# Queries and keys turned by VectorE and a round trip through HBM, in place of TensorE transposes, in an encoder block

## The chip, the cores and the metric

The kernel runs on one core of a Trainium2 chip, in float32, in one launch. The metric is the device time of one execution in microseconds (us). The median of three runs before the change is 1106.71 us (1106.16 to 1112.32).

Engines are named as in the profile: PE is TensorE (matrix products and transposes), DVE is VectorE, ACT is ScalarE, POOL is GpSimd, SP is SyncE. SP and POOL mostly issue DMA transfers here. Each engine runs its instructions in the order of the program, and waits at an instruction until the data and buffers that it needs are there.

## The reference

The reference is one layer of an encoder for 512 tokens of width 1024. It consists of a half-step feed-forward block, a mixing block with two branches, and a second half-step feed-forward block:

```python
x = x + FFN_RES * _swiglu(_rmsnorm(x, norm_ffn1[l]), w_ffn1_gu[l], w_ffn1_down[l])
h = _rmsnorm(x, norm_mix[l])
xr, gr, q, k, v, ga, gb = jnp.split(h @ w_in[l], splits, axis=-1)
xc = _centred_dwconv(xr, conv_w[l], conv_b[l])
h_fwd = _rglru_scan(xc, ...)            # a recurrence over the tokens, with sigmoid gates
h_bwd = jnp.flip(_rglru_scan(jnp.flip(xc, 1), ...), 1)
y_lru = (h_fwd + h_bwd) * jax.nn.gelu(gr)
q = _rmsnorm(q.reshape(B_, S, N_HEADS, HEAD_DIM), q_norm[l]) * (HEAD_DIM ** -0.5)
k = _rmsnorm(k.reshape(B_, S, N_HEADS, HEAD_DIM), k_norm[l])
y_att = _neighbourhood_attention(q, k, v, rpb[l])   # 16 heads of 64, on an 8 x 64 token grid
y = jax.nn.sigmoid(ga) * y_lru + jax.nn.sigmoid(gb) * y_att
x = x + y @ w_out[l]
x = x + FFN_RES * _swiglu(_rmsnorm(x, norm_ffn2[l]), w_ffn2_gu[l], w_ffn2_down[l])
```

In the attention each token sees a clamped window of 8 rows by 16 columns. A block of 16 query columns is treated against 32 key columns: scores, a bias that also masks, softmax, and the weighted sum of v.

## The kernel before

**Weights and products.** A product in float32 is made of three products of parts: each operand is cut into a high part (a cast) and a low part (the rest). A weight chunk of 128x1024 is loaded by SP into one of three buffers (`wraw`), cut by a cast on ACT (`wh`, line 145; for some chunks on DVE, line 147) and a subtraction on DVE (`wl`, line 148), with four buffers each for `wh` and `wl`, and used by 24 matmuls of 128x512. A merge-gate chunk whose number is odd has its cast on DVE (`f % 2 == 0` in `gates`).

**Order of the work.** PE's order is set by the weight chunks: after (and in the middle of) a chunk `weave` is called, which takes steps from lists of generators, the lanes. A table `RATE` says how many steps of a lane are due per call in each phase. The lanes are `lru` (the recurrence, by a list of numbered steps), `v` (copies of v), `att` (the attention, `heads`) and `tail` (the last applications). `hold` puts an instruction behind the last matmul of the chunk that is current when the step is taken. Within this a scheduler orders each engine's instructions, with `high_priority` for some. The phases are `xr` (input of the recurrence), `t0` (q, k and v of the first eight heads, `hf` 0), `t1` (the same for `hf` 1) and `g` (24 chunks of gates: gelu gate, merge gate A, merge gate B). The first attention half so runs beside the q, k and v chunks of the second, and the second beside the gates.

**q and k.** `tok_group` makes q or k for 128 tokens on the partitions and 512 features: four accumulators (`acc`), four chunks. `qk_raw` copies them from the accumulators on ACT (line 843) into `qk` tiles and takes the sums of squares. In `heads` DVE multiplies by the reciprocal root (line 909). `start(fi)` then handles a pair of heads (`fi` 0 to 3 per half): PE transposes four 128x128 blocks of q (line 918) and four of k (line 920) into `aux` accumulators, ACT makes the scaled high parts `qh` and `kh` (lines 924 and 927), DVE the low parts `ql` and `kl` (lines 926 and 929).

**Scores, softmax, weights.** `scores` issues 12 matmuls (64x256) for one group of query blocks, 24 where both groups are taken together (line 950). DVE adds the bias and takes the minimum of the negated scores (line 970, result `nmx`), ACT the exponentials with their sums (line 977), DVE the reciprocal (line 979) and the multiplication by it (line 982). `ship` turns the weights in 32x32 blocks on DVE (lines 991 and 992) into `pt`, SP stores that to HBM (`pd`), and POOL fetches it back in four transfers into `PT` (line 998). This completes a transposition. `apply` multiplies `PT` with v in 32 matmuls (line 1013). It runs a few units behind: `ATT_LAG` is 4 units for `hf` 0 and 2 for `hf` 1, where a unit is 12 matmuls of scores in `hf` 0 and 24 in `hf` 1.

**v.** v is stored to HBM (`vd`) and fetched back by POOL in shifted forms: `vs` (line 869), and for two edge blocks `va` and `ve` (line 880), six pieces of 64 KB per block, gathered in runs of 64 numbers. `apply` of a half needs all of them.

## Time and profile before

| | before |
|---|---|
| median of 3 runs | 1106.71 us |
| profiled execution | 1114.74 us |
| its span | 1113.0 us |
| granted TensorE clock, mean | 0.995 |
| PE busy | 1102.2 us (99%) |
| DVE busy | 813.4 us (73%) |
| ACT busy | 578.1 us (52%) |
| POOL busy | 148.9 us (13%) |
| bytes moved by DMA | 175.93 MB, 158 GB/s |

The profiled execution took 8.0 us longer than the median; 1.7 us of its time lie outside the span. The busy time of PE counts a matmul from its start to its modelled end, and neighbouring matmuls overlap in it. So a PE that is busy 99% of the time is one that hardly ever has nothing to do, and the time can fall only where PE gets less to do, or where its few idle stretches go. The attention runs beside the chunks from the first transpose at 508.8 us to the end of the last application at 691.4 us of the span.

### The profile page before, as it was taken

How to read it: one execution, taken by the hardware profiler on the slowest of the kernel's cores; microseconds unless marked ns; L12 is line 12 of the kernel's file. 1: busy time of each engine (PE TensorE's matmuls, PEld its weight loads, DVE VectorE, ACT ScalarE, POOL GpSimd, SP SyncE). 2: the span in 40 equal slices, each digit the busy share in tenths (PEclk: the TensorE clock that was granted, in tenths of full speed). 3: DMA queues.
4: the chain of work that ended last, by engine and by line, in shares of the span. 5: the costliest groups of instructions: out<-in, count | busy, mean ns of one | idle time of the engine just before them, and what ended most of it. 6: DMA issues, size and time to landing. Idle time of an engine off the chain costs nothing.

```text
span 1113.0 us, 17676 instructions
## 1 busy us (share of the span) xinstructions
PE 1102.2 (99%) x6811; PEld 976.0 (88%) x6811; DVE 813.4 (73%) x1295; ACT 578.1 (52%) x871; POOL 148.9 (13%) x243
## 2 busy tenths in 40 slices
PE   9999999999999999999999998999999999999998
PEld 7899999988888778788888876889999999998887
DVE  7877777794745776999787974659877777785542
ACT  8554554563533678877354441346655454564330
POOL 0000000000000351230335432001000000000000
PEclk9999999999999999999999998999999999999999
DMA  8566666643423696673796665377766666662421
GB/s 267 154 168 152 155 154 166 165 139 95 134 85 108 166 245 156 173 206 116 205 258 183 205 186 137 101 239 161 198 146 160 157 166 148 158 170 95 133 76 38
DMA packets 64549, 175.93 MB, mean 158 GB/s; under 512 B 14545, under 2 KB 18385, under 8 KB 64465
## 3 DMA queue, kind: packets, MB, share of 16 engines
q1 hardware_dynamic: 43136, 127.75, 35.8%
q0 software_dynamic: 20752, 46.80, 21.5%
q8 instruction: 53, 0.87, 0.3%
q10 hardware_dynamic: 576, 0.26, 0.1%
q14 instruction: 32, 0.25, 0.1%
HBM read 150.53 MB, written 15.73 MB: 149 GB/s over the span
## 4 chain that ended last, share of the span: by engine, by line
PE 95%; issue 2%; DMA 1%; POOL 1%; DVE 0%; ACTq 0%; POOLq 0%; ACT 0%
PE acc L312 31%; PE acc L172 10%; PE acc L173 10%; PE acc L174 10%; PE aux L312 5%; PE acc L831 4%; PE acc L832 4%; PE acc L833 4%; PE aux L172 4%; PE aux L174 4%; PE aux L173 4%; PE aux L742 1%; DMA PT<-pd 1%; POOL PT L998 1%; PE aux L1013 1%
## 5 line engine op out<-in xcount | busy, mean ns | idle before, releaser
L145 ACT ACTIVATE wh<-wraw 128x1024 fp32r<-128x1024 f32 (+3 forms) x224 | 220.7, 987 | 303.7 <-issue 92.1
L148 DVE TENSOR_TENSOR wl<-wraw,wh 128x1024 fp32r<-128x1024 f32 (+3 forms) x236 | 267.3, 1137 | 101.4 <-ACT wh L145 100.3
L312 PE MATMUL acc<-s,wh 128*128 128x256 f32 x1280 | 232.2, 283 | 0.0
L312 PEld LDWEIGHTS acc<-s,wh 128*128 128x128 f32 x1280 | 199.7, 192 | 0.0
L312 PE MATMUL acc<-s,wl 128*128 128x256 f32 x640 | 181.1, 283 | 0.0
L312 PEld LDWEIGHTS acc<-s,wl 128*128 128x128 f32 x640 | 122.9, 192 | 0.0
L172 PE MATMUL acc<-xh,wh 128*128 128x512 f32 x272 | 108.7, 400 | 0.0
L174 PE MATMUL acc<-xh,wl 128*128 128x512 f32 x272 | 107.0, 393 | 0.0
L173 PE MATMUL acc<-xl,wh 128*128 128x512 f32 x272 | 106.9, 393 | 0.0
L312 PE MATMUL acc<-xh,wl 128*128 128x256 f32 x320 | 90.6, 283 | 0.0
L312 PE MATMUL acc<-xl,wh 128*128 128x256 f32 x320 | 90.6, 283 | 0.0
L312 PE MATMUL acc<-xh,wh 128*128 128x256 f32 x320 | 90.5, 283 | 0.0
L831 PE MATMUL acc<-wh,xh 128*128 128x512 f32 x192 | 75.7, 394 | 0.0
L832 PE MATMUL acc<-wh,xl 128*128 128x512 f32 x192 | 74.8, 389 | 0.0
L833 PE MATMUL acc<-wl,xh 128*128 128x512 f32 x192 | 74.7, 389 | 0.0
L148 DVE TENSOR_TENSOR hl<-h,hh 128x512 fp32r<-128x512 f32 x88 | 57.2, 686 | 21.7 <-PE aux L173 21.4
L172 PE MATMUL aux<-hh,wh 128*128 128x512 f32 (+1 forms) x181 | 69.9, 386 | 0.0
L173 PE MATMUL aux<-hl,wh 128*128 128x512 f32 (+1 forms) x181 | 69.9, 386 | 0.0
L174 PE MATMUL aux<-hh,wl 128*128 128x512 f32 (+1 forms) x181 | 69.9, 386 | 0.0
L173 PE MATMUL acc<-hl,wh 128*128 128x512 f32 (+1 forms) x176 | 67.9, 386 | 0.0
L174 PE MATMUL acc<-hh,wl 128*128 128x512 f32 (+1 forms) x176 | 67.9, 386 | 0.0
L172 PE MATMUL acc<-hh,wh 128*128 128x512 f32 (+1 forms) x176 | 67.9, 386 | 0.0
(221 smaller groups left out, 2297.6 us busy)
## 6 DMA issues: line engine op xcount, KB each, us to landing
wraw<-wqkv SPq DMA_DIRECT2D x24, 512.0 KB, 4.9
wraw<-wg SPq DMA_DIRECT2D x24, 512.0 KB, 7.5
wraw<-w1d SPq DMA_DIRECT2D x22, 512.0 KB, 3.7
wraw<-w2s SPq DMA_DIRECT2D x22, 512.0 KB
pair<-w2s SPq DMA_DIRECT2D x22, 512.0 KB, 4.5
wraw<-w2d SPq DMA_DIRECT2D x22, 512.0 KB, 3.7
wraw<-w1s SPq DMA_DIRECT2D x18, 512.0 KB, 3.6
pair<-w1s SPq DMA_DIRECT2D x18, 512.0 KB, 4.9
```

Of the source, the lines that this page charges most:

```text
L145: nc.scalar.activation(H, raw, AF.Copy)
L148: return nc.vector.tensor_tensor(L, raw, H.bitcast(F32), ALU.subtract)
L172: nc.tensor.matmul(ps, wh, xh, start=first, stop=False, skip_group_check=skip)
L173: nc.tensor.matmul(ps, wh, xl, start=False, stop=False, skip_group_check=skip)
L174: mark["mm"] = nc.tensor.matmul(ps, wl, xh, start=False, stop=last, skip_group_check=skip)
L312: mm = nc.tensor.matmul(o, w_[:, c], x_, start=first and m + k == 0 and w_ is H and x_ is xh_, stop=m + k == 4 and w_ is L, skip_group_che ...
L742: prev, mm = mm, nc.tensor.matmul(ps[d][b], W[w][o, c], X[x][o], start=x == 1, stop=w + x == 0)
L831: nc.tensor.matmul(pss[j], xh[kk][:, tj], H[:, s], start=kk == 0, stop=False)
L832: nc.tensor.matmul(pss[j], xl[kk][:, tj], H[:, s], start=False, stop=False)
L833: mark["mm"] = nc.tensor.matmul(pss[j], xh[kk][:, tj], L[:, s], start=False, stop=kk == KT - 1)
L998: nc.gpsimd.dma_start(PT[:, j].rearrange("p q i -> p (q i)"), d[q].rearrange("i c x -> c i x"))
L1013: mm = nc.tensor.matmul(pv[h2 * HD : (h2 + 1) * HD, n * P : (n + 1) * P], vt[:, (fi * 2 + h2) * HD : (fi * 2 + h2 + 1) * HD], PT[:, q], st ...
```

## The change

Five things change together.

1. q and k are no longer turned by PE. A new lane `prep` (`turn_qk`) normalises a tile of q and of k and turns each in 32x32 blocks on DVE into a `pair` tile, which SP stores to HBM (`qd`, four stores of 512 KB per half, in rows of 4 KB). Its steps are due at 1.25 per call in the phases `t0`, `t1` and `g`, so they fall between v's weight chunks. `fetch(qd, fi)` reads a pair of heads back in four transfers on SP (32 partitions by 16 runs of 64 numbers each), into one of two `xqk` buffers. `start(fi)` first issues the fetch for `fi + 1`, and then makes `qh`, `ql`, `kh`, `kl` from `xqk`. The 64 transposes of PE are gone.
2. The norm weight of k is multiplied into that of q (`gq8`), so `kh` and `kl` are made without a scale.
3. The multiplication of the softmax weights by 1/sum moves from DVE to ACT.
4. The casts of all merge-gate and gelu-gate chunks are on ACT; before, every second one was on DVE.
5. The pool of large tiles goes from 43 to 39, and some tiles take other buffers (`ch`, `cl` and part of `th` those of `PT` and `xqk`, `sq` that of `pt`). The rate of `lru` in `t0` goes from 3.25 to 3.

```diff
 RATE = {
-    "t0": {"att": 0.0, "lru": 3.25},
-    "t1": {"att": 0.75, "tail": 0.75, "lru": 2},
-    "g": {"att": 0.7, "tail": 0.7, "lru": 1.5, "v": 0.5},
+    "t0": {"att": 0.0, "lru": 3, "prep": 1.25},
+    "t1": {"att": 0.75, "tail": 0.75, "lru": 2, "prep": 1.25},
+    "g": {"att": 0.7, "tail": 0.7, "lru": 1.5, "v": 0.5, "prep": 1.25},
 }
...
-    gk = small[:, C_KN : C_KN + 1]
+    nc.vector.tensor_tensor(gq8, gq8, small[:, C_KN : C_KN + 1], ALU.mult)
...
-    def heads(hf, raws, st):
+    def turn_qk(raws, st, qd, ahead):
...
-        for w in range(2):
-            for j in range(NCB):
+        for j in range(NCB):
+            t2 = pair_t().rearrange("p a b -> p (a b)")
+            for w in range(2):
                 t = raws[w][j].rearrange("p (h d) -> p h d", d=HD)
                 hold(nc.vector.tensor_tensor(t, t, rq[:, w, j, :].unsqueeze(2).to_broadcast([P, 8, HD]), ALU.mult))
+                nc.vector.transpose(
+                    t2.rearrange("p (c f w i) -> p w f c i", c=NCB, f=4, w=2)[:, w],
+                    raws[w][j].rearrange("p (f c i) -> p f c i", c=NCB, i=32))
+            nc.sync.dma_start(qd[j], t2)
+            yield
+        if ahead:
+            fetch(qd, 0)
+
+    def fetch(qd, fi):
+        t = xs[fi] = big.tile([P, NCB * NCB, 2, 32], F32, tag="xqk", bufs=2, name=nm("xqk"))
+        for c in range(NCB):
+            nc.sync.dma_start(
+                t[c * 32 : (c + 1) * 32].rearrange("p g w i -> p g (w i)"),
+                qd.rearrange("j (a i) c f x -> c f i (j a) x", a=NCB)[c, fi])
+
+    def heads(hf, qd):
+        until("prep", lambda: False)
+        if 0 not in xs:
+            fetch(qd, 0)
             yield
...
         def start(fi):
-            fs = slice(fi * P, (fi + 1) * P)
-            pq, pk = aux_t(), aux_t()
-            for j in range(NCB):
-                hold(nc.tensor.transpose(pq[:, j * P : (j + 1) * P], raws[0][j][:, fs], ident))
-            for j in range(NCB):
-                hold(nc.tensor.transpose(perm(pk)[:, j], raws[1][j][:, fs], ident))
+            if fi < 3:
+                fetch(qd, fi + 1)
+            x = xs.pop(fi).rearrange("p (j a) w i -> p w j a i", j=NCB)
+            xq, xk = x[:, 0], x[:, 1]
...
-            nc.scalar.activation(rev(qh), fwd(pq), AF.Copy, scale=gq8)
+            hold(nc.scalar.activation(rev(qh), xq, AF.Copy, scale=gq8))
...
-            nc.scalar.activation(kh, pk, AF.Copy, scale=gk)
+            hold(nc.scalar.activation(rows(kh), xk, AF.Copy))
             with tc.high_priority():
-                mark["kl"] = nc.vector.scalar_tensor_tensor(kl, pk, gk, kh.bitcast(F32), ALU.mult, ALU.subtract)
+                mark["kl"] = nc.vector.tensor_tensor(rows(kl), xk, rows(kh.bitcast(F32)), ALU.subtract)
...
-                    nc.vector.tensor_scalar(pt, pt, rs[:, hp, n : n + 1], None, ALU.mult)
+                    nc.scalar.activation(pt, pt, AF.Copy, scale=rs[:, hp, n : n + 1])
...
-        lanes["att"].append(heads(hf, raws, st))
+        qd = dram.tile([NCB, P, NCB, 4, 64], F32, tag="qd", bufs=2, name=nm("qd"))
+        lanes["prep"].append(turn_qk(raws, st, qd, hf == 0))
...
+        lanes["att"].append(heads(hf, qd))
...
-            feat_chunk(a["wg3"][w * KT + f], KT, xh, xl, ps, 0, KT, f % 2 == 0, RATE[phase[0]])
+            feat_chunk(a["wg3"][w * KT + f], KT, xh, xl, ps, 0, KT, True, RATE[phase[0]])
```

How this moves the instructions is shown at three places. Numbers at the end of names are those of the tiles.

**First place: PE at the first scores of `hf` 0.** Before, the eight transposes of the first pair of heads (`aux_5186` for q, `aux_5187` for k) are followed by a weight chunk (`wh_5207`), and the scores come behind that:

```order
L918 MATMUL aux_5186<-ident,qk_4444 128x128
L918 MATMUL aux_5186<-ident,qk_4446 128x128
L920 MATMUL aux_5187<-ident,qk_4625 128x8x16
L920 MATMUL aux_5187<-ident,qk_4627 128x8x16
L920 MATMUL aux_5187<-ident,qk_4629 128x8x16
L920 MATMUL aux_5187<-ident,qk_4631 128x8x16
L831 MATMUL acc_5119<-wh_5207,xh_3096 128x512
L832 MATMUL acc_5119<-wh_5207,xl_3097 128x512
```

Now the end of a weight chunk (`wh_5155`) is followed at once by the scores, 24 in a row:

```order
L834 MATMUL acc_4961<-wh_5155,xh_3102 128x512
L835 MATMUL acc_4961<-wh_5155,xl_3103 128x512
L836 MATMUL acc_4961<-wl_5156,xh_3102 128x512
L975 MATMUL aux_5088<-kl_5044,qh_5041 128x256
L975 MATMUL aux_5087<-kl_5044,qh_5041 128x256
L975 MATMUL aux_5088<-kh_5043,qh_5041 128x256
L975 MATMUL aux_5087<-kh_5043,qh_5041 128x256
```

No weight chunk now lies between the work on q and k and the scores; and two units of scores stand together where before a chunk stood between them.

**Second place: ACT at the same point.** Before, the parts of the first pair are made between two weight casts, and then the exponentials of the first unit follow:

```order
L145 ACTIVATE wh_5432<-wraw_5431 128x1024
L924 ACTIVATE qh_5196<-aux_5186,gq_3677 128x4x128
L927 ACTIVATE kh_5198<-aux_5187,small 128x512
L145 ACTIVATE wh_5529<-wraw_5528 128x1024
L977 ACT_TABLE_LOAD
L977 ACTIVATE p_5251,rs_5236<-so_5253,nmx_5254 128x192
```

Now two casts stand directly ahead of `qh` and `kh`. `wh_5467` takes the buffer of `wh_5155`, the chunk that PE uses last before the scores:

```order
L145 ACTIVATE wh_5390<-wraw_5389 128x1024
L145 ACTIVATE wh_5467<-wraw_5466 128x1024
L949 ACTIVATE qh_5041<-xqk_5001,gq_3677 128x4x128
L952 ACTIVATE kh_5043<-xqk_5001 128x4x8x16
L1002 ACTIVATE p_5101,rs_5086<-so_5103,nmx_5104 128x192
L1002 ACTIVATE p_5102,rs_5086<-so_5103,nmx_5104 128x256
```

Behind the four exponentials and four multiplications of that unit come the parts of the second pair, two tanh of the recurrence, and only then the copies out of the accumulators that `wh_5155`'s chunk filled; PE's next chunk writes to these accumulators:

```order
L1007 ACTIVATE p_5101<-p_5101,rs_5086 128x192
L1007 ACTIVATE p_5102<-p_5102,rs_5086 128x256
L949 ACTIVATE qh_5136<-xqk_5036,gq_3677 128x4x128
L952 ACTIVATE kh_5138<-xqk_5036 128x4x8x16
L769 ACTIVATE th_5149<-gate_4806,sp_3673 128x512
L769 ACTIVATE th_5152<-gate_4815,sp_3673 128x512
L846 ACTIVATE qk_5184<-acc_4958 128x512
```

The softmax of a unit has moved ahead of the copies that free the accumulators.

**Third place: POOL in the second half of the attention.** Before, the copies of v's edge blocks (`va`, `ve`) for `hf` 1 stand ahead of its softmax weights (`PT`), but for one piece:

```order
L876 MEMSET ve_6123 128x512
L880 DMA va_6122<-vd_82 64x4x64 x2
L880 DMA ve_6123<-vd_82 64x4x64
L880 DMA va_6122<-vd_82 64x4x64 x2
L998 DMA PT_6017<-pd_6015 128x1x224 x4
L880 DMA ve_6123<-vd_82 64x4x64
L892 DMA bm_6549<-rpb 128x640
L892 DMA bm_6551<-rpb 128x640
L998 DMA PT_6310<-pd_6308 128x1x224 x4
```

There `PT_6017` is the last of `hf` 0 and `PT_6310` the first of `hf` 1. Now the first `PT` of `hf` 1 (`PT_6101`, `PT_6111`) stand between those copies, and the last two pieces stand behind those of the next pair of heads (`PT_6310`, `PT_6320`):

```order
L879 MEMSET ve_6410 128x512
L883 DMA va_6409<-vd_82 64x4x64 x2
L883 DMA ve_6410<-vd_82 64x4x64
L883 DMA va_6409<-vd_82 64x4x64
L1023 DMA PT_6310<-pd_6308 128x1x224 x4
L1023 DMA PT_6320<-pd_6318 128x1x224 x4
L883 DMA va_6409<-vd_82 64x4x64
L883 DMA ve_6410<-vd_82 64x4x64
```

From the first `PT` of `hf` 1 to the last piece of v that its first application needs, POOL now issues 16 transfers of `PT`, the twelve pieces of `va` and `ve`, one `vs` and two `bm` in a row; before, one piece of v stood behind a `PT` transfer, and that one was of `hf` 0.

23 lines of the change are left out of this document (14 added, 9 removed).

## The prediction

> **What bounds the kernel now.** I read the page first: the busy times and the chain that ended last.
>
> ```profile
> PE 1102.2 (99%) x6811; PEld 976.0 (88%) x6811; DVE 813.4 (73%) x1295; ACT 578.1 (52%) x871; POOL 148.9 (13%) x243
> PE 95%; issue 2%; DMA 1%; POOL 1%; DVE 0%; ACTq 0%; POOLq 0%; ACT 0%
> ```
>
> PE bounds it: 99% busy, and 95% of the chain. DVE at 73% and ACT at 52% have slack on average. So the time changes by what PE no longer does, and by the waits of PE that go or come. The view of waits, for PE alone, shows which there are:
>
> ```profile
> PE aux L1013 <- DMA PT<-pd: 5.8, 2, 3.7
> ```
>
> That is 5.8 us in 2 waits, the longest 3.7 us, both of an application for softmax weights (`PT`) still on their way. A table by stretches (columns: length, busy time and count of PE, PEld, DVE, ACT and POOL, granted clock, DMA share, GB/s) shows what follows on each:
>
> ```profile
> 600.00:605.00 5.00, 5.00 (x43) 3.88 (x43) 1.36 (x2) 1.28 (x2) 1.72 (x4) 1.00 0.57 172
> 640.00:645.00 5.00, 2.87 (x30) 2.49 (x27) 3.46 (x18) 3.34 (x14) 1.73 (x3) 0.85 0.91 284
> 645.00:650.00 5.00, 5.00 (x20) 4.06 (x19) 2.94 (x6) 2.33 (x5) 1.97 (x3) 0.81 0.44 127
> 685.00:690.00 5.00, 1.31 (x22) 1.07 (x19) 1.78 (x3) 0.00 (x0) 0.00 (x0) 0.79 0.55 147
> 690.00:695.00 5.00, 5.00 (x23) 3.95 (x20) 1.29 (x2) 1.63 (x3) 0.00 (x0) 0.53 0.00 0
> ```
>
> After each wait the clock is below 1.00: 0.53 over the 5 us behind the 3.7 us wait, which loses 0.47 x 5 = 2.35 us. I price the slow clock behind a wait of 2 us and more at 2.4 us. The two waits so cost 5.8 + 2 x 2.4 = 10.6 us.
>
> The work of PE in the chain of waits (start, length, what), at full clock:
>
> ```profile
> 508.55 0.23 PE acc L833
> 508.79 0.44 PE aux L918 x4
> 509.23 0.44 PE aux L920 x4
> 556.97 1.90 PE aux L1013 x32
> 605.19 0.94 PE aux L950 x12
> 606.13 0.74 PE acc L950 x12
> ```
>
> A chunk matmul takes 0.23 us, so a chunk of 24 takes 5.5 us; scores of 24 take 1.7, an application 1.9, four transposes 0.44.
>
> **The change part by part.** *Transposes.* 16 groups of four leave PE: 16 x 0.44 = **-7.0 us**, all on the path. The work goes to DVE and SP, which the waits of PE do not name.
>
> *DVE and ACT.* Their costs per instruction, from the groups of the attention's stretch (busy, mean ns, idle before), the first three from the groups of the whole span:
>
> ```profile
> L145 ACT ACTIVATE wh<-wraw 128x1024 fp32r<-128x1024 f32 (+3 forms) x224 | 220.7, 987 | 303.7 <-issue 92.1 <-PE acc L312 73.5 <-PE acc L173 72.5
> L766 ACT ACTIVATE th<-gate,sp 128x512 f32<-128x512 f32 x16 | 11.3, 719 | 0.0
> L843 ACT ACTIVATE qk<-acc 128x512 f32<-128x512 f32 x16 | 9.0, 592 | 1.9 <-PE acc L833 1.8
> L977 ACT ACTIVATE p<-so,nmx 128x256 f32<-128x256 f32 x32 | 15.9, 497 | 5.8 <-DVE nmx L970 5.7
> L977 ACT ACTIVATE p<-so,nmx 128x192 f32<-128x192 f32 x32 | 14.3, 446 | 18.9 <-DVE nmx L970 18.9
> L977 ACT ACTIVATION_READ_ACCUMULATOR p<-so,nmx 128x1 f32 x64 | 12.0, 187 | 0.0
> L977 ACT ACT_TABLE_LOAD x4 | 5.1, 1283 | 2.6 <-DVE nmx L970 2.6
> L927 ACT ACTIVATE kh<-aux,small 128x512 fp32r<-128x512 f32 x8 | 5.4, 676 | 1.0 <-PE aux L920 1.0
> L924 ACT ACTIVATE qh<-aux,gq 128x512 fp32r<-128x512 f32 x8 | 5.4, 672 | 2.3 <-PE aux L918 2.3
> L992 DVE STREAM_TRANSPOSE pt<-p 128x512 f32<-128x512 f32 x16 | 10.9, 682 | 0.0
> L982 DVE TENSOR_SCALAR p<-p,rs 128x256 f32<-128x256 f32 x32 | 11.2, 351 | 0.1
> L982 DVE TENSOR_SCALAR p<-p,rs 128x192 f32<-128x192 f32 x32 | 10.2, 318 | 0.2
> L147 DVE CAST wh<-wraw 128x1024 fp32r<-128x1024 f32 x11 | 7.8, 710 | 13.2 <-PE acc L173 12.1 <-PE acc L832 1.0
> L929 DVE SCALAR_TENSOR_TENSOR kl<-aux,small,kh 128x512 fp32r<-128x512 f32 x8 | 5.9, 741 | 0.9 <-ACT kh L927 0.9
> L970 DVE CUSTOM_DVE_ANT_0 so<-aux,bm 128x256 f32<-128x256 f32 x24 | 10.0, 415 | 0.0
> ```
>
> DVE gains 32 block transposes (nearest row 0.68 us: +21.8) and loses the multiplications by 1/sum (11.2 + 10.2 = 21.4) and 12 casts (12 x 0.71 = 8.5): -8 in sum. ACT gains 64 multiplications, which no row shows; the bound below is DVE's 0.33, above the exponential's 0.47, and I take 0.45, so +29, and 12 casts of 0.99: +12. These sums lie beside PE's work and cost nothing as such. What counts is where they stand in the queues, by the three places shown above.
>
> *First scores of `hf` 0 (wait 1).* PE now comes to the scores right after the chunk of `wh_5155`. They need `kl_5044`. On ACT `kh_5043` stands behind `wh_5467`, which cannot start until PE has read `wh_5155` for the last time. From the end of that chunk: cast 0.99, `qh` 0.67, `kh` 0.68, `kl` 0.74 = 3.1 us in which PE has nothing. Before, a chunk of 5.5 us covered all but the cast. More if `xqk` is not there by then: the last store and the fetch are two DMA trips in a row, and nothing shows when they start. The rows of the queues give landing times (KB each, median us):
>
> ```profile
> wraw<-wqkv SPq DMA_DIRECT2D x24, 512.0 KB, 4.9
> pd<-pt SPq DMA_DIRECT2D x16, 448.0 KB, 6.3
> PT<-pd POOLq DMA_DIRECT2D x64, 112.0 KB, 5.3
> va<-vd POOLq DMA_DIRECT2D x16, 64.0 KB, 3.7
> ```
>
> 6.3 + 5.3 = 11.6 us from the store's issue, two chunks' time. I estimate the store at one to two chunks before the scores, so 0 to 4 us more; I take 1.
>
> *The copies behind them (wait 2).* PE's next chunk writes to accumulators that `qk_5184` must copy out first. On ACT that copy stands behind four exponentials (2 x 0.50 + 2 x 0.45 + 4 x 0.19 = 2.6), four multiplications (1.8), `qh` and `kh` (1.35), two tanh (1.4) and, where the table has to be changed, a load of 1.28; the copy takes 0.6. That is 7.8 to 9.1 us after the first minimum is there, some 1.4 us after the scores began (0.94 of PE, 0.4 of DVE). PE's scores take 1.7, so it waits 7.5 to 8.8; I take 8. Two waits beyond 2 us: 2 x 2.4 more. First scores together: 3.1 + 1 + 8 + 4.8 = **+17**.
>
> *First scores of `hf` 1.* In the order `qh_5985` stands there behind such a cast too (of the chunk that PE ends last), with the scores next on PE: 3.1 + 2.4 = **+5.5**; up to 9 with a late fetch.
>
> *POOL (wait at the first application of `hf` 1).* Its timeline (start, busy us, what, idle before):
>
> ```profile
> 598.41 1.59 POOL L880 DMA_DIRECT2D va<-vd  x2
> 601.67 0.77 POOL L880 DMA_DIRECT2D ve<-vd  x1 [1.67 <-issue]
> 604.06 1.95 POOL L880 DMA_DIRECT2D va<-vd  x2 [1.62 <-issue]
> 647.19 1.97 POOL L998 DMA_DIRECT2D PT<-pd  x3 [3.94 <-issue]
> 651.74 2.10 POOL L998 DMA_DIRECT2D PT<-pd  x3 [2.59 <-issue]
> 678.31 2.09 POOL L998 DMA_DIRECT2D PT<-pd  x3 [2.52 <-issue]
> 683.24 1.32 POOL L998 DMA_DIRECT2D PT<-pd  x2 [2.84 <-issue]
> ```
>
> POOL issues three `PT` in 2 us and then stands for 2.5 to 4, held by nothing that the profile shows: 4.6 us from 647.19 to 651.74 and 4.9 from 678.31 to 683.24, about 1.6 us each. The `va` and `ve` go at (604.06 - 598.41) / 3 = 1.9. So from the first `PT` of `hf` 1 to the last piece of v, 16 x 1.6 + 12 x 1.5 (below 1.9, since some go in the pauses of others) + 3 for the rest = 47 us, and 3.7 to landing. POOL begins about 13 us after `hf` 1's first scores (exponentials and turns, some 6, and 6.3 for the store). That makes 64 us. PE gets from those scores to the last matmul of that application with three scores (5.1), two and a half applications (4.7) and 113 chunk matmuls (26): 36 us. The difference is 28. Against it stands that POOL's busy time alone, 0.67 per `PT` and 0.8 per piece, is 23, with which the wait would be 4. I take **+20**, with the slow clock of its parts in it, since the pauses may shrink when landings are quicker; both ends stay in the range.
>
> *The end of the attention.* From the last scores to the last application PE has the same 25 us as before, and the wait of 3.7 stays, with its clock: **+6** against the two old waits (10.6), which I take out.
>
> A rule of the Trainium skill bears on the clock: "TensorE: Matmul & The Clock Gate", Part 1, has the half clock come after an idle window of about 3.4 us. By it the waits of 3.1 us would keep the full clock and the sum be 5 us less. The trace differs: behind the shorter of the two waits, 5.8 - 3.7 = 2.1 us, the table shows 0.81, so I keep the price.
>
> **The sum.** -7.0 - 10.6 + 17 + 5.5 + 20 + 6 = +31. The profiled execution took 1114.7 us, 8 above the median of 1106.7; on the median this makes 1138 us.
>
> **The rivals.** *A: POOL is quick enough.* If the pauses on POOL come from slow landings at a DMA share of 0.9, and the application finds its v after 4 us, the sum is +31 - 16 = +15: 1122. For it speaks the small busy time, against it that the pauses are as long at 678 us as at 651.
>
> *B: the queues at the first scores do not hold, and faster.* The one mechanism here is the release of DVE: with 8 us less to do and no accumulator of PE to wait for, the weights (`pt`) of each unit leave earlier, so both old waits go and POOL's work starts earlier. Then only the shortest queue remains, 3.1 us at each of the two first scores without a slow clock, with the copies covered by ACT's slack (it is 48% idle): -7.0 - 10.6 + 6.2 = -11, so 1095. It decides if `qk_5184` comes within 2 us of the scores' end. ACT's order speaks against it.
>
> *C: fetches on SP hold the weights.* SP issues 16 fetch transfers and stores ahead of weight loads. A fetch reads runs of 256 bytes; the row with such runs, `va`, takes 3.7 us for 64 KB, where 512 KB in long rows take 4.9. If a fetch of four transfers of 128 KB takes 4 x 3.7 = 15 us in place of 5.3, the first scores and the `hf` 1 ones wait some 10 more each: 1158. "DMA: Bandwidth & Descriptors", Specifications, of the Trainium skill names 512 bytes as the least for full rate, which points the same way; no row here has a fetch of that size in such runs.
>
> **How the numbers follow.** The forecast has 0.48, A 0.20, B 0.20, C 0.12. Between the bounds of its terms (POOL 4 to 28, fetch 0 to 4, copies 7.5 to 8.8) the forecast goes from 1122 to 1150. The range takes in A and most of B and C: 1097 to 1158. A measurement here can tell about 1% from no change (11 us). Faster by more needs less than 1095.6: some 0.6 of B and nothing else, 0.12. Within 1%, up to 1117.8: the rest of B and the lower half of A, 0.18. Slower 0.70.
>
> **What would show it.** Right: PE's waits name ACT or DVE at the first scores of each half (line 975) and the accumulators' copies at the chunk behind (line 846), with 3 and 8 us; at the first application of `hf` 1 (line 1038) they name DMA `va`, `ve` or `PT`, 10 us or more in one or two waits; the clock drops behind each. PE's busy time falls by about 7. A is shown by an application that waits under 5 us, B by a PE without waits above 2 us at line 975, C by DMA `xqk` as what the first scores wait for. The forecast is wrong if ACT works through its queue at the first scores in less than 4 us, or if the tail of the attention ends where it did.

## The result and the profile after

The changed kernel takes 1158.47 us (median of four runs, 1155.62 to 1160.47), the kernel before 1109.5 us beside it (four runs, 1106.16 to 1112.32). The ratio is 1.0441, with a 95% interval of 1.0395 to 1.0487. The profiled execution took 1155.62 us with a span of 1153.8 us, 40.8 us more than the span before; its mean granted clock is 0.978 (0.995 before).

The page gives PE as busy as before, and less of the chain to it:

```profile
PE 1102.0 (96%) x6747; PEld 973.7 (84%) x6747; DVE 800.3 (69%) x1236; ACT 619.7 (54%) x950; POOL 148.0 (13%) x243
PE 80%; DVE 7%; DMA 4%; issue 4%; ACT 3%; POOL 2%; SPq 0%; DVEq 0%; POOLq 0%; ACTq 0%
```

64 transposes are gone (6747 matmuls and transposes in place of 6811), yet the busy time fell by only 0.2 us, and the rest of the span grew by 41. The view of PE's waits (total, times, longest) says where:

```profile
PE aux L975 <- DVE kl L954: 21.6, 2, 13.3
PE aux L1038 <- DMA va<-vd: 17.1, 3, 10.1
PE acc L834 <- ACT qk L846: 7.0, 1, 7.0
PE aux L1038 <- DMA PT<-pd: 0.8, 1, 0.8
PE acc L834 <- DVE v L859: 0.7, 1, 0.7
```

Without the start of the program these are 47.2 us, against 6.1 before. The places are the forecast ones: the first scores of both halves, the chunk behind those of the first, and the first application of the second half. The table by stretches (columns as in the prediction) shows the clock falling at each:

```profile
490.00:500.00 10.00, 9.10 (x41) 7.20 (x39) 10.00 (x14) 5.08 (x7) 4.04 (x6) 1.00 0.90 289
500.00:510.00 10.00, 2.52 (x24) 2.52 (x24) 5.97 (x8) 1.24 (x2) 5.84 (x8) 0.67 0.77 152
510.00:520.00 10.00, 3.01 (x10) 2.23 (x9) 5.65 (x21) 9.05 (x23) 1.17 (x2) 0.50 0.41 105
590.00:600.00 10.00, 0.00 (x0) 0.00 (x0) 1.74 (x2) 0.65 (x1) 2.10 (x4) 0.61 1.10 249
650.00:660.00 10.00, 1.81 (x8) 1.15 (x7) 2.02 (x8) 2.29 (x7) 4.04 (x7) 0.85 0.60 167
```

The chain of waits (start, length, what) shows what stands in the first two of these waits, and in the second half's:

```profile
493.42 6.58 DMA qd<-pair
...
501.45 3.76 DMA xqk<-qd
...
505.32 0.73 ACT qh L949
...
506.83 0.60 DVE kl L954
507.43 1.14 DVE th L787
508.56 1.13 DVE th L789
...
510.71 1.48 ACT p L1002 x6
...
515.64 1.23 ACT th L769 x2
516.87 0.49 ACT qk L846
...
585.64 6.38 DMA qd<-pair
...
593.63 4.97 DMA xqk<-qd
```

In the first half the last store goes out at 493.4 us and `qh` starts at 505.3: the trip takes 11.9 us, 6.6 for the store and 5.3 for the fetch, while PE had 5.7 us of work left (until 499.1). The copy that PE needs next ends at 517.4, behind the exponentials and the tanh, as the order had said. In the second half the store goes out at 585.6, and ScalarE's timeline has `qh` at 600.9, after 10.2 us of nothing (in brackets the idle time before, and what ended it):

```profile
507.48 0.58 PE L975 MATMUL aux<-kl,qh 64*128 64x256 f32 x2 [8.38 <-DVE kl L954]
505.32 0.72 ACT L949 ACTIVATE qh<-xqk,gq 128x512 fp32r<-128x512 f32 x1 [5.35 <-DMA xqk<-qd]
600.88 0.72 ACT L949 ACTIVATE qh<-xqk,gq 128x512 fp32r<-128x512 f32 x1 [10.24 <-DMA xqk<-qd]
```

That is 15.2 us, 6.4 for the store and 8.8 for the fetch, of which PE had work for 4. PE's view names VectorE (`kl`) for both waits, because `kl` is the last step; ScalarE, one step ahead of it, stood 15.6 us for the fetch in these two places.

### The profile page after: what moved, and what is told of

The parts are those of the page before. It is cut to its first block, busy times and chain, and to the rows that moved or that the text cites. A ratio compares the mean times of both kernels' runs of the same rounds, so it can differ in the third digit from the quotient of the medians.

```text
span 1153.8 us, 17649 instructions
## 1 busy us (share of the span) xinstructions
PE 1102.0 (96%) x6747; PEld 973.7 (84%) x6747; DVE 800.3 (69%) x1236; ACT 619.7 (54%) x950; POOL 148.0 (13%) x243
## 4 chain that ended last, share of the span: by engine, by line
PE 80%; DVE 7%; DMA 4%; issue 4%; ACT 3%; POOL 2%; SPq 0%; DVEq 0%; POOLq 0%; ACTq 0%
PE acc L312 30%; PE acc L172 8%; PE acc L174 8%; PE acc L173 8%; PE aux L312 5%; PE aux L172 4%; PE aux L173 4%; PE aux L174 4%; PE acc L834 2%; PE acc L835 2%; PE acc L836 2%; DVE wl L148 1%; DMA qd<-pair 1%; POOL PT L1023 1%; DMA pd<-pt 1%
## 5 line engine op out<-in xcount | busy, mean ns | idle before, releaser
L145 ACT ACTIVATE wh<-wraw 128x1024 fp32r<-128x1024 f32 (+3 forms) x236 | 233.4, 991 | 325.6 <-PE acc L173 95.6
```

The costliest lines, as they stand in the source:

```text
L145: nc.scalar.activation(H, raw, AF.Copy)
```

## The experiments

All runs of the kernel before beside these lie between 1104.7 and 1113.0 us. A single run so says little about 5 us and less; the waits in its profile say more. Each row below is one run unless it says otherwise, and then the time is the median. "Waits" is the sum of PE's waits in the profiled run but for the first, at the program's start.

| run | us | waits, us | clock |
|---|---|---|---|
| kernel before (profile) | 1114.7 | 6.1 | 0.995 |
| changed kernel (profile) | 1155.6 | 47.2 | 0.978 |
| `turn_only` | 1150.8 | 42.2 | 0.979 |
| `act_parts_timed` (12 runs; profile) | 1111.0 | 5.6 | 0.998 |
| `no_trip` | 1159.3 | 46.6 | 0.974 |
| `rows_no_trip` | 1156.8 | 47.0 | 0.979 |
| `no_store` | 1154.5 | 39.1 | 0.976 |
| `light` | 1142.3 | 31.9 | 0.984 |
| `first_pe` | 1152.4 | 38.2 | 0.982 |
| `first_pe_all` (4 runs) | 1144.9 | 36.8 | 0.982 |
| `v_early` | 1148.7 | 43.6 | 0.982 |
| `later_v` | 1140.2 | 30.7 | 0.985 |
| `gap_v` | 1140.6 | 31.7 | 0.985 |
| `gap_hp` | 1134.8 | 29.7 | 0.989 |
| `ring_after` | 1152.1 | 44.2 | 0.979 |
| `ring_gap` | 1117.6 | 14.4 | 0.992 |
| `light_gap` | 1116.5 | 13.2 | 0.993 |
| `ring_gap_p` (4 runs) | 1119.7 | 16.8 | 0.992 |
| `ring_before` (10 runs) | 1104.4 | 0 | 1.000 |

**Which part costs: the turning or ScalarE's new work.** One part alone on the kernel before, and one part undone in the changed kernel. On the kernel before (`act_parts`, later timed as `act_parts_timed`):

```diff
-                    nc.vector.tensor_scalar(pt, pt, rs[:, hp, n : n + 1], None, ALU.mult)
+                    nc.scalar.activation(pt, pt, AF.Copy, scale=rs[:, hp, n : n + 1])
...
-            feat_chunk(a["wg3"][w * KT + f], KT, xh, xl, ps, 0, KT, f % 2 == 0, RATE[phase[0]])
+            feat_chunk(a["wg3"][w * KT + f], KT, xh, xl, ps, 0, KT, True, RATE[phase[0]])
```

> The kernel before, with only the two shifts to ScalarE: the multiplication by 1/sum and the casts of all gate chunks. Transposes stay on TensorE. Theory (the turning of q and k is what costs; the shifts to ScalarE are hidden): within 8 us of the kernel before, 1100 to 1117, the waits of TensorE at most 3 us above those before (5.8). Rival (ScalarE becomes the engine that is waited for): the softmax weights come later, the late waits grow to 12 us or more, 1117 to 1130.

> The kernel before with only the two shifts to ScalarE, timed: one look gave 1108.6 beside 1107.7. Theory (both are hidden beside TensorE's work): the ratio to the kernel before is between 0.995 and 1.003. Rival (VectorE's 30 us less take out part of the late waits of 10.6 us): 0.988 to 0.995.

The single run gave 1108.6 us; over twelve, the ratio is 1.0022 (1.0007 to 1.0037). The two shifts are hidden there, and gain nothing. `turn_only` makes the same edit backwards in the changed kernel:

> The changed kernel with the two shifts to ScalarE undone: the multiplication by 1/sum and every second gate cast are on VectorE again; q and k are turned by VectorE and the trip through HBM. Theory (the trip and the order around it cost, not the shifts): 1150 to 1165, with the waits for kl above 18 us and those at the first application of the second half above 10. Rival (with ScalarE less loaded the copies and parts come earlier): the 7.0 us for the copies go below 4 and the time falls to 1140 to 1150.

1150.8 us. The waits, as PE's view gives them:

```profile
PE aux L975 <- DVE kl L954: 27.7, 2, 18.7
PE acc L834 <- ACT qk L846: 5.2, 1, 5.2
```

The wait for the copies got 1.8 us shorter, with four multiplications less ahead of them on ScalarE (the rival asked for under 4); that for `kl` got 6 longer; and va's fell from 17.1 to 6.8, against the expectation. The time is at the edge between theory and rival, some 8 us below the changed kernel, so the shifts may cost a few us there. The other 42 us over the kernel before come without them: turning q and k is what costs. The smaller parts that go with it (the smaller pool of large tiles, the other buffers, the rate of `lru`) were not tried apart.

**What the first scores wait for.** `no_trip` takes the wait for the stores out of the first fetch, by fetching other data:

```diff
+    other = a["wqkv"][0].rearrange("j p (c f x) -> j p c f x", c=NCB, f=4)
...
-                qd.rearrange("j (a i) c f x -> c f i (j a) x", a=NCB)[c, fi])
+                (other if fi == 0 else qd).rearrange("j (a i) c f x -> c f i (j a) x", a=NCB)[c, fi])
+            after(ld, mark["store"])
```

The last line keeps SyncE's order as it was (`ld` is the fetch, `mark["store"]` the last store).

> The changed kernel in which the first pair of heads of each half is fetched from a weight input instead of from the q and k just stored, so that this fetch waits for no store; every instruction keeps its place in the order of its engine. The attention of pairs 0 and 4 so works on other numbers. Theory (the trip through HBM is what the first scores wait for): the two waits for kl at the first scores, 21.6 us together, fall to the queue on ScalarE and VectorE, 3 to 4.5 us each, 6 to 9 together; the slow clock behind the second of them gets shorter; the time falls by 12 to 18 us, to about 1140. Rival (the queues on ScalarE and VectorE are the wait, the trip is hidden behind them): the waits stay above 18 us and the time within 5 us of the changed kernel.

The theory missed: 1159.3 us, and

```profile
PE aux L978 <- DVE kl L957: 18.2, 2, 12.1
```

Issued right behind the store at 493.7, the fetch had landed at 502.9; in the second half it went out at 584.8 and was used at 598.4. Without having to wait for the stores it took 9.2 and 13.6 us. The numbers are those of the rival, but not its reason: of the 18.2 us ScalarE stood 12.1 for this fetch. Having to wait for the store is not what makes the trip long; while the store is under way the fetch takes nearly as long as both. `rows_no_trip` then made its runs long:

```diff
-                (other if fi == 0 else qd).rearrange("j (a i) c f x -> c f i (j a) x", a=NCB)[c, fi])
+                other.rearrange("j (f i) c g x -> f i j (c g x)", f=4)[fi][:, c] if fi == 0 else
+                qd.rearrange("j (a i) c f x -> c f i (j a) x", a=NCB)[c, fi])
```

> As the run without the trip (first pair of each half fetched from a weight input, not from the stored q and k), and this fetch in addition reads long rows, 32 of 4 KB per transfer in place of 512 runs of 256 bytes, so that the rearrangement of the first pair is left out too; same bytes, same order of every engine. In the run without the trip the waits for kl were still 18.2 us, with the fetch taking 9.2 us and 13.6 us from its first issue to the first use. Theory A (the short runs are what makes the fetch slow): the fetch takes under 6 us, the waits for kl fall to the queue on ScalarE and VectorE, 6 to 8 us together, the time to 1140 to 1148. Theory B (the DMA engines are simply full with weights, stores and fetches at that time, and the length of runs does not matter): the waits stay above 14 us, the time within 5 us of 1159.

Theory B: 1156.8 us, 22.1 us of waits for `kl`. So runs of 256 bytes, on which rival C of the prediction rested, are not the reason. `no_store` leaves the stores out as well:

```diff
-            nc.sync.dma_start(qd[j], t2)
...
-                qd.rearrange("j (a i) c f x -> c f i (j a) x", a=NCB)[c, fi])
+                other.rearrange("j (a i) c f x -> c f i (j a) x", a=NCB)[c, fi])
```

> As the run without the trip, but all pairs are fetched from the weight input and the eight stores of turned q and k are left out, so 4 MB less is written and nothing of them stands ahead of the fetch in SyncE's queue of transfers; TensorE, ScalarE and VectorE keep their order. Theory (the fetch is slow because it queues behind the stores and loads that were issued just before it): the first fetch of each half takes under 6.5 us from its first issue to the first use, in place of 9.2 and 13.6, the waits for kl fall from 18.2 to under 12 us, the time to 1142 to 1152. Rival (other traffic, above all GpSimd's copies of v and the softmax weights, fills the DMA engines): the fetch stays above 8 us, the waits above 15 us, the time within 5 us of 1158.

```profile
PE aux L977 <- DVE kl L956: 9.9, 2, 5.6
```

```profile
583.52 14.08 SPq L928 DMA_DIRECT2D xqk<-wqkv  x9
593.26 0.72 ACT L951 ACTIVATE qh<-xqk,gq 128x512 fp32r<-128x512 f32 x1 [2.61 <-DMA xqk<-wqkv]
```

The waits for `kl` fell to 9.9 us, as the theory had it, but the fetch did not get as short as it asked: in the second half it took 9.8 us from the first issue (583.5) to the first use (593.3), in place of 13.6 and not under 6.5. In the first half SyncE issued it 6 us earlier than in `no_trip` (487.8), before the last tiles were turned, so there the run says nothing of its length. So in the second half some 4 us are the stores ahead of the fetch. What holds the other 9.8 is not shown: weight loads and GpSimd's transfers went on, and the DMA share was still 1.06 over 590 to 600 us. The time, 1154.5, is the rival's, since the other waits stayed. Of the 9.9 us left, the first wait, 4.3, is the queues on ScalarE and VectorE, which the prediction had at 3.1; the second, 5.6, has 2.6 us of ScalarE standing for the fetch in it. `light` leaves out three of four fetches too:

```diff
     def fetch(qd, fi):
+        if fi:
+            xs[fi] = xs["last"]
+            return
```

> The changed kernel with almost all of the added traffic left out: no stores of turned q and k, one fetch per half in place of four, from a weight input; all pairs work on these numbers. All work on VectorE and ScalarE is kept. Theory (the added traffic fills the DMA engines and delays the rest): the waits for kl fall to the queues, under 10 us, those for v and softmax weights from 17.9 to under 9, the time to 1120 to 1138. Rival (places in queues and GpSimd's pauses, not bytes): kl under 10 as in the run without stores, but the others stay above 14, the time 1145 to 1156.

1142.3 us, between the two: `kl` 8.3 us, the v pieces 12.4. Its fetches still took 8 to 10.5 us to land, with no store of q and k ahead of them; they were issued early enough that ScalarE stood 1.2 us for them. Bytes matter, but a good part of the wait for v is not bytes.

`first_pe` takes the other way and lets PE turn the first pair of each half:

```diff
+            if fi == 0:
+                pq, pk = aux_t(), aux_t()
+                for p_, w in ((pq, 0), (pk, 1)):
+                    for j in range(NCB):
+                        hold(nc.tensor.transpose(p_[:, j * P : (j + 1) * P], raws[w][j][:, :P], ident))
```

> The changed kernel with one part undone: the first pair of heads of each half is turned by TensorE again (16 of the 64 transposes, 1.8 us), the other three pairs take the trip through HBM. Theory (the first scores wait because the trip is longer than what TensorE has left to do): the waits for kl at the first scores fall from 21.6 us to under 3; those for the copies (7.0) and for pieces of v (17.1) stay or grow by what moves earlier; 1128 to 1142. Rival (the trip of the second pair, or the full DMA engines, make the same wait one unit later): waits for kl or the copies of 15 us or more, above 1145.

The waits for `kl` by stretches, 480 to 545, 545 to 610 and 660 to 740 us:

```profile
PE aux L977 <- DVE kl L956: 0.7, 1, 0.7
PE aux L977 <- DVE kl L956: 5.3, 1, 5.3
PE aux L977 <- DVE kl L956: 2.1, 1, 2.1
```

At the first scores of the two halves they fell from 21.6 to 0.7 us, as the theory had it: the 5.3 stand at the second pair of the second half (601.4 us; its first scores began at 580.9 without a wait), and the 2.1 at the fourth. So the first scores waited for the trip. The time fell only to 1152.4, as the rival had it: in part the wait comes back one pair later, 3.6 us are waited for the tiles that PE turns, and the wait for v's pieces is 18.2.

**The copies of v on GpSimd.** `v_early` raises the rate of their lane:

```diff
-    "g": {"att": 0.7, "tail": 0.7, "lru": 1.5, "v": 0.5, "prep": 1.25},
+    "g": {"v": 2.0, "att": 0.7, "tail": 0.7, "lru": 1.5, "prep": 1.25},
```

> The changed kernel with the lane of v's copies at 2 steps per call in place of 0.5, and first in the list, in the phase of the gates; this puts all pieces of v for the second half ahead of its softmax weights on GpSimd. Theory (the application waits for pieces queued behind softmax weights): the 17.1 us waited for va at the applications go, less than 4 us are left there, and with the slow clock the time falls by 15 to 22 us, to 1134 to 1143. Rival (GpSimd is short of time as a whole, so that the wait only moves to the softmax weights): the waits at the applications stay above 10 us, now for PT, and the time falls by less than 8.

```profile
PE aux L975 <- DVE kl L954: 30.6, 3, 16.6
...
PE aux L1038 <- DMA PT<-pd: 2.8, 2, 2.4
```

The 17.1 us are gone, as expected; but the time fell by only 10 us to 1148.7, because the waits for `kl` grew by 9: the second half's last store went out at 589.2 us, 3.5 later than in the changed kernel, and its fetch was used at 605.1. Whether the early pieces of v did that was not tried apart.

**Putting the queues right, one after another.** `later_v` adds pauses of the attention lane to `v_early`: one in the first half and two in the second behind the fetch, and as many behind `start(0)`. `gap_v`, shown here, puts all of them between fetch and parts:

```diff
             fetch(qd, 0)
             yield
+        for _ in range(2 if hf == 0 else 4):
+            yield
```

> As the run with early v, and in addition the attention lane pauses between the first fetch and the first pair's parts, and between these and the first scores: one step each for the first half, two steps each for the second. On TensorE two more weight chunks stand ahead of the first scores of the first half, and about two and a half ahead of those of the second. Theory (all of the loss are waits at three places, each of which can be covered by chunks): the waits for kl go from 21.6 to under 4 us, those at the chunk behind (7.0) to under 2, and the time falls below the kernel before by the 7 us of transposes and part of its late waits: 1090 to 1105. Rival (the second half's attention, pushed back, ends too late): the last applications wait 5 to 15 us for softmax weights, 1110 to 1125. Rival (the added traffic and ScalarE's 41 us more slow the whole stretch): above 1125.

> As the run with later scores and early v, but the pauses of the attention lane all lie between the first fetch and the first pair's parts (two steps in the first half, four in the second). On ScalarE the copies out of the accumulators so stand ahead of the parts of the first pair, while in the run with later scores they stood behind parts that waited for the fetch, and TensorE waited 9.5 us for them. Theory (ScalarE stands at an operation whose data are on their way, and what is behind it waits too): the wait for the copies falls from 9.5 us to under 2, the time from 1140 to 1122 to 1132. Rival (ScalarE is too busy there in any order): another wait of 5 us or more for ScalarE takes its place within 20 us, the time stays above 1135.

`later_v` came out at 1140.2 us, far above its theory: no wait for `kl` is left, but 9.5 us for the copies behind parts whose data were on the way. `gap_v` removed exactly that and took no less, 1140.6:

```profile
PE acc L834 <- ACT wh L145: 15.5, 1, 15.5
PE aux L1040 <- DMA PT<-pd: 11.9, 4, 6.4
```

The time is the rival's, the reason is not: the new wait ends at 549.3 us, 41 us behind the old one, and is for a weight part whose load came late. It stood on SyncE behind 16 fetches and three stores of softmax weights, which wait for VectorE. `gap_hp` puts the loads ahead:

```diff
+        with tc.high_priority():
             ld = nc.sync.dma_start(raw[:, s], src[:, s])
```

> As the run with the pause behind the fetch, with one thing more: the loads of weights have high priority, so they stand in SyncE's queue ahead of fetches and of stores of softmax weights when their buffers are free. In the run with the pause TensorE waited 15.5 us for a weight part whose load stood behind 16 fetches and three stores. Theory (weights held on SyncE): that wait falls below 3 us and the time from 1140 to 1115 to 1125, with about 12 us for softmax weights left. Rival (the fetches, pushed behind the weights, are late instead): the waits for kl or for copies rise by 10 us or more, the time stays above 1133.

The 15.5 us are gone, and the time is 1134.8 us, short of what was expected, as the wait for softmax weights grew to 16.1 and one for v's eviction came up. The rival's time came, but not its waits for `kl` or copies:

```profile
PE aux L1041 <- DMA PT<-pd: 16.1, 3, 10.8
PE acc L173 <- DVE v L860: 8.0, 1, 8.0
```

`first_pe_all` combines the first pair on PE with early v and early loads, and makes the next pair's parts later:

```diff
-            if 0 in n2s:
+            if 1 in n2s:
                 if fi < 3:
                     start(fi + 1)
+            if 0 in n2s:
```

> As the run with the first pair on TensorE, with three more: the copies of v early, the weight loads at high priority on SyncE, and the parts of the next pair made after the second group of scores in place of the first, so that ScalarE's copies out of the accumulators stand ahead of them. Theory (every loss is a place in a queue): no wait of TensorE above 6 us, waits below 20 us in all, 1105 to 1120. Rival (GpSimd's rate of transfers is the next bound): one or two waits for softmax weights of 8 us or more, 1115 to 1130. In no case below the kernel before by more than the 5 us that 48 transposes are worth.

1144.9 us, ratio 1.0315 (1.0294 to 1.0336). Expectation and rival both missed; 16.4 us are waits for softmax weights, 11.0 for `kl`, 6.8 for the copies. At this point each queue had been put right once, and 30 to 37 us were still waited.

**GpSimd's pauses.** Open were the traffic and the pauses of GpSimd that the prediction had priced but not explained. `ring_after` doubles the buffer for GpSimd's descriptors in the changed kernel, `ring_gap` in `gap_hp`:

```diff
-    NBIG = 39
+    NBIG = 38
...
-    nc = bacc.Bacc("TRN2", target_bir_lowering=False, num_devices=1, dynamic_dma_scratch_size=2048)
+    nc = bacc.Bacc("TRN2", target_bir_lowering=False, num_devices=1, dynamic_dma_scratch_size=4096)
```

> The changed kernel with GpSimd's descriptor buffer doubled (4096 in place of 2048 bytes per partition), for which the pool of large tiles gives one (38 in place of 39); GpSimd's order is the same. Theory (GpSimd pauses after about three transfers because its descriptors are used up until earlier transfers land): pauses come after about six, the 43 us from the first softmax fetch of the second half to the last piece of v become 25 to 33, the waits for va (17.1 us) fall below 8, the time falls by 8 to 18 us to 1140 to 1150. Rival (the pauses are the full DMA engines, not the buffer): the 43 us stay above 38, the time within 5 us of 1158.

> The run with the pause and early weights, with GpSimd's descriptor buffer doubled in the same way. There 16.1 us of waits for softmax weights were left. Theory (GpSimd's pauses are the next bound): these fall below 7 us and the time from 1135 to 1115 to 1125. Rival (the DMA engines): within 5 us of 1135.

GpSimd's timeline in the changed kernel, from the first `PT` of the second half to the last piece of v:

```profile
616.89 2.03 POOL L1023 DMA_DIRECT2D PT<-pd  x3 [6.01 <-DMA pd<-pt]
620.93 0.66 POOL L1023 DMA_DIRECT2D PT<-pd  x1 [2.00 <-issue]
...
629.55 2.05 POOL L1023 DMA_DIRECT2D PT<-pd  x3 [2.97 <-issue]
634.27 0.80 POOL L883 DMA_DIRECT2D ve<-vd  x1 [2.67 <-issue]
...
659.94 0.78 POOL L883 DMA_DIRECT2D ve<-vd  x1
```

and the same stretch in `ring_after`:

```profile
626.12 2.69 POOL L1023 DMA_DIRECT2D PT<-pd  x4 [5.05 <-DMA pd<-pt]
...
633.26 2.69 POOL L1023 DMA_DIRECT2D PT<-pd  x4 [1.83 <-DMA pd<-pt]
...
655.70 0.78 POOL L883 DMA_DIRECT2D ve<-vd  x1
```

43 us became 30, the groups of three became groups of four with no pause inside, and the wait for va fell from 17.1 to 7.4 us. Of the pauses left there, three of under 1 us are put down to landings of GpSimd's own transfers (`vs`, `PT`, `va`), as the theory has it. The time fell by 6 us, less than the 8 to 18 expected, as the waits for `kl` stood at 26.8 in this run. In `ring_gap` the softmax weights are not waited for any more, and the time is 1117.6 us:

```profile
PE acc L173 <- DVE v L860: 7.3, 1, 7.3
PE aux L978 <- DVE kl L957: 3.9, 2, 3.5
```

`light_gap` leaves the added traffic out of `gap_hp` instead, by the edits of `light`:

> The run with the pause and early weights, with almost all of the added traffic left out as in the light run. Theory (the added traffic): the waits for softmax weights fall from 16.1 to under 6 us, the time to 1105 to 1118. Rival (GpSimd): they stay above 11 us, the time above 1125.

1116.5 us, 3.9 us for softmax weights. Both help alike: with less traffic what GpSimd sent lands sooner, with more buffer it needn't wait for that. The two theories were no alternatives; that both of them name one cause is how I read it, not a run by itself.

`ring_gap_p` was to take the wait for v's eviction:

```diff
-    "t1": {"att": 0.75, "tail": 0.75, "lru": 2, "prep": 1.25},
+    "t1": {"att": 0.75, "tail": 0.75, "lru": 2, "prep": 0.5},
```

> The run with the pause, early weights and doubled descriptor buffer (1117.6 us in one look), with the lane that turns q and k at 0.5 in place of 1.25 steps per call while the second half's v chunks run. VectorE so has about 4.5 us less ahead of v's eviction, for which TensorE waited 7.3 us. Theory (queue on VectorE): that wait falls to 2 to 4 us, the ratio to the kernel before is 1.000 to 1.007. Rival (the stores of the second half come later and with them the first scores): a wait for kl of 6 us or more, 1.008 to 1.015. The 7 us of transposes bound what it can gain: not below 0.995.

It did not: 7.8 us there, 5.7 for `kl`, and 1119.7 us, a ratio of 1.0101 (1.0072 to 1.0129), which is in the rival's band. And `ring_before` gives the larger buffer to the kernel before (pool of large tiles 42):

> The kernel before with only GpSimd's descriptor buffer doubled (pool of large tiles 42 in place of 43); TensorE's, GpSimd's and SyncE's order is the same. Theory (its two late waits, 5.8 us with 4.8 of slow clock, are GpSimd's pauses): they go, and the ratio to the kernel before is 0.990 to 0.996. Rival (they are the store's landing): 0.997 to 1.002.

1104.4 us, a ratio of 0.9969 (0.9959 to 0.9979), between the theory's band and the rival's, and the fastest of all. The waits decide for the theory, as its PE is busy without one but the first:

```profile
PE 1097.7 (100%) x6811; PEld 973.1 (88%) x6811; DVE 812.4 (74%) x1295; ACT 578.3 (52%) x871; POOL 149.2 (14%) x243
```

The group of the `PT` fetches shows the pauses of the kernel before (idle before, "issue"):

```profile
L998 POOL DMA_DIRECT2D PT<-pd x64 | 43.3, 681 | 111.3 <-issue 62.8 <-DMA pd<-pt 40.7 <-PE acc L174 4.0
```

and that they are nearly gone in `ring_before`, where 2.9 us of "issue" in 3 pauses are left of 62.8 in 28:

```profile
L998 POOL DMA_DIRECT2D PT<-pd x64 | 43.4, 688 | 99.8 <-DMA pd<-pt 65.2 <-PE acc L950 10.8 <-PE aux L950 7.4
```

## Why the prediction was wrong

Direction and places were right, the size was not: +31 us forecast, +40.8 in the spans of the two profiles and +49 in the medians, just outside the range.

- **Failed: the first scores, "I estimate the store at one to two chunks before the scores, so 0 to 4 us more; I take 1", and for the second half "3.1 + 2.4".** Measured are 8.4 and 13.3 us of waiting in place of 4.1 and 3.1, 14.5 us too little. The prediction took ScalarE's and VectorE's queues for the wait, and the trip through HBM for nearly covered. The runs show the trip: without it for the first pair (`first_pe`) these waits are 0.7 us. The store went out 5.7 and 4.1 us before PE was out of work, at the lower end of my estimate and below. In the first half the trip took 11.9 us, where I had summed 11.6; with one chunk of 5.5 us to cover it, and `qh`, `kh` and `kl` behind it, that sum gives 11.6 - 5.5 + 2.1 = 8.2 us, what was measured. So the numbers were there, and the 1 and the 4 did not follow from them. In the second half the fetch took 8.8 us in place of 5.3, and the trip 15.2. Why is open in part: neither the wait for the store (`no_trip`) nor the short runs (`rows_no_trip`) make it slow, the stores ahead of it some 4 us (`no_store`), and the rest was not taken apart.
- **Near in size, partly by luck: the copies behind the first scores.** 7.0 us against 8, at the place that was named. But the first minimum came 3.2 us after the scores began (1.4 forecast), because VectorE first did three operations of the recurrence (lines 787, 789 and 793); from there the first copy ended after 6.7 us (7.8 to 9.1 forecast), and the scores took 2.9 us at the slow clock (1.7 forecast). These errors cancel.
- **Right in place, near in size: GpSimd.** It began 13.8 us after the scores (13 forecast) and took 43 us (47 forecast). From the scores to the last of these waits went 59 us, in which PE had 42 us of work; the working had 64 and 36. PE waited 17.1 us for pieces of v, with the slow clock near the 20 forecast. The 20 itself was chosen between 28 and 4, so that it came near is luck in part. The doubt kept with it, that quicker landings shorten the pauses, is what `light_gap` and the ring runs show.
- **Wrong, small: the end of the attention.** Forecast +6 with a wait of 3.7 us; 0.8 were left.
- **Half right: the clock.** It fell behind the waits, as forecast. But PE's busy time stayed, where a fall by about 7 us had been named as a sign; as I read it, the slow clock took back what the transposes gave, since more was waited. How much of the 7 us was gained can't be read from any run: `ring_gap` has 1096.8 us busy at a clock of 0.992, `ring_before` 1097.7 at 1.000. The price of 2.4 us was also worked out for the longer of the old waits alone; around the shorter one the two rows shown lose (0.15 + 0.19) x 5 = 1.7 us.
- **Wrong, without weight: VectorE's gain.** There are 16 block transposes of 0.70 us, not 32, so by the prediction's own sum VectorE loses 19 us and not 8 (its busy time fell by 13.1). Rival B leaned on this release; it did not come even so.
- **The basis.** The profile before, at 1114.7 us, was longer than any of its timed runs (1104.7 to 1113.0), the profile after at 1155.6 the shortest of its four. Of the 18 us between +31 and +49, 8 are this, and 10 the sum.
- **Rivals.** A (the application finds its v) and B (faster) did not come. C named the place that failed, and its sign came one engine removed: ScalarE waited for `xqk`, and PE for `kl` behind it. Its reason, the short runs, is excluded by `rows_no_trip`; that its 1158 is the measured time is chance.

By `gap_hp` and `ring_gap`, which differ in the buffer, one us waited costs (1134.8 - 1117.6) / (29.7 - 14.4) = 1.1 us, slow clock included. Taken down to no wait, the reordered kernel would end near 1101 us, 3 below `ring_before`: an estimate, from two single runs, of what is in the idea at most. Left open is which order reaches it.

## What to carry to other kernels

Taking work from the engine that bounds a kernel gains only its time there; what replaces it must be timed from its last producer to its first use, and compared with the work that the bounding engine has in between: here 12 and 15 us against 5.7 and 4.1. A view of waits names the last step only; look one engine further back for what that step stood for. Where engines run in order, one operation whose data are late holds everything queued behind it (here copies, weights and v), and a wait taken away in one queue came back in the next, until GpSimd's pauses were shortened or its competing traffic was left out. Idle time that a profile puts down to nothing ("issue") is worth an experiment before any reordering: a larger buffer took 17 us from the reordered kernel (one run each) and 3 from the kernel before.

## What the runs showed of the hardware

GpSimd's pauses were nearly all those of its descriptor buffer: with 2048 bytes per partition it issued up to three transfers of softmax weights and then stood, for 2.2 us on average in the kernel before (62.8 us in 28 pauses); with 4096 bytes it issued four to seven transfers in a row, 0.67 us for each of softmax weights. The Trainium skill ("DMA: Bandwidth & Descriptors", SWDGE vs HWDGE vs iDMA) describes that GpSimd writes descriptors to rings in a part of SBUF, from which the DMA engines drain them. The runs agree, in that a larger buffer takes the pauses away (2.9 us are left of the 62.8 in the kernel before); that GpSimd stands when there is no room is how I read them. With more in flight each transfer lands later: the median for a `PT` went from 4.6 us in the changed kernel to 5.8 in `ring_after`, from 4.5 in `gap_hp` to 6.5 in `ring_gap`, and from 5.3 to 5.6 in the kernel before.

A fetch of 512 KB took 9 to 14 us from issue to use when it was sent right behind a store and a weight load of the same size, whether its runs were 256 bytes or 4 KB. Sent only after the store had landed, it took 5.3 us in the first half of the changed kernel and 8.8 in the second; with no store ahead of it, still 9.8 (`no_store`, second half).

The clock stood at 0.50 to 0.85 in the stretches of 10 us with waits that are shown above, and at 1.00 in 490 to 500 us, ahead of them. A short wait was enough: in the kernel before, 1 us at a time, it was 0.50 from 644 to 646 us, behind a wait of 2.1 us that ended at 642.4, and 1.00 again from 647 us.
